# A row-sum kernel on one core: its first 8 MB loaded by two DMAs of 64 partitions instead of one of 128

## The chip, the core and the metric

The kernel runs on one core of a Trainium2 chip. The time is the device time of one execution in microseconds (us), the median of three runs. VectorE is DVE in the profile, ScalarE is ACT, GpSimd is POOL, SyncE is SP, and SyncE's queue of DMA issues is SPq. TensorE is not used.

## What is computed

```
x: [32, 512, 1024] float32
relu_x = np.maximum(x, 0)
return np.sum(relu_x, axis=-1)        # [32, 512] float32
```

That is 16,384 rows of 1,024 numbers, 67.1 MB in, and one number per row out, 65.5 KB.

## The kernel before

The rows are laid on the 128 partitions of the on-chip memory. A partition takes 16 consecutive rows at a time, which is one contiguous stretch of 64 KB in DRAM. Seven loads of 8 MB (128 stretches of 64 KB each, `ROWS = 16`) go in turn into three buffers (`NBUF = 3`, tiles `io0` to `io2`). A last block of 8 MB comes in smaller loads: 8 rows per partition, 4 rows, and then four rows cut into pieces that get smaller towards the end.

All loads are issued by SyncE (helper `load`, line 103), in order, on its one queue. From the fourth on, a load waits until VectorE has finished with the buffer that it overwrites (the tuple in `freed`). Each load has a semaphore of its own, which stands at 16 once its data are there.

The first block is worked on in the simplest way: ScalarE loads its activation table (line 142) and clamps the whole buffer in place (`clamp`, line 144), then VectorE sums all its rows (`total`, line 152). The table load carries ScalarE's wait for the first load. Later blocks are cut in two halves of 8 or 7 rows for these two steps, and from the sixth block on some rows are done in one instruction each, which clamps and sums: on ScalarE (`act_row`, line 159) or on VectorE (`dve_row`, line 167). The last four rows are shared out by columns among ScalarE, VectorE and GpSimd (lines 121, 126, 234, 254).

The sums gather in the tile `res`, one column per row of a partition. Three stores, all on SyncE's queue behind the loads (helper `store`, wait at line 114, issue at line 115), bring them out: the first block's 16 columns, all the others but two, and the last two.

The order of instructions is written out by hand: there is no scheduler. `open_without_barrier` takes the first `EARLY` instructions of SyncE, which are loads, and puts them into the program's opening block, ahead of all else that SyncE does. At the end SyncE clears the semaphores.

The first block has its own views of the arrays, `xf` and `of`; all other blocks use `xv` and `ov`. In both, partition p holds 16 consecutive rows.

Of the kernel before, what the change touches and what calls it, by code (L numbers as in the profile page):

```python
# [5 lines left out]
RELU = mybir.ActivationFunctionType.Relu  # L6
MAX, ADD = mybir.AluOpType.max, mybir.AluOpType.add
P = 128

ROWS = 16  # L10
NBUF = 3
# [13 lines left out]
LAST_DVE, LAST_ACT = 252, 151  # L25
MIDDLE_ACT, END_ACT = 214, 321

EARLY = 1


def kernel(tc: tile.TileContext, x: bass.AP, out: bass.AP):
    nc = tc.nc
    sems = Semaphores(tc)

    tc.close()
    tc.compile()
    nc.cur_bb = nc.bb_map[tc.start_bb_name]
    body = nc.cur_bb.bb.instructions
    ends = list(body)
    body.clear()  # L40
    n_stores = relu_sum(nc, sems, x, out)
    body.extend(ends)


    nc.cur_bb = nc.bb_map[tc.start_bb_name + "_end"]
    nc.cur_bb.bb.instructions.clear()
    nums = sorted(s.num for s in (*sems.loads, sems.act, sems.dve))
    cleared = range(nums[0], nums[-1] + 1)
    assert len(cleared) == len(nums)
    nc.sync.sem_clear(cleared)  # L50
    nc.sync.wait_ge(sems.stored, 16 * n_stores).then_inc(sems.stored, -16 * n_stores)
    open_without_barrier(tc, EARLY)


class Semaphores:
    def __init__(self, tc: tile.TileContext):
        n = len(TWO) + len(TAIL) + 4
        self.loads = [tc.alloc_semaphore(f"load{i}") for i in range(n)]
        self.act = tc.alloc_semaphore("act")
        self.dve = tc.alloc_semaphore("dve")  # L60
        self.end = self.loads[-1]
        self.stored = tc.alloc_semaphore("stored")


def relu_sum(nc, sems: Semaphores, x: bass.AP, out: bass.AP):
    x_flat = x.flatten_outer_dims()
    N, D = x_flat.shape
    NT = N // P
    NB = len(TWO)
    assert N == P * NT == P * ROWS * (NB + 1)  # L70
    assert sum(TAIL) == ROWS - 4
    assert HEAD + MIDDLE + LAST_DVE == D and HEAD == 2 + LAST_DVE

    bufs = [nc.alloc_sbuf_tensor(f"io{i}", [P, ROWS, D], F32) for i in range(NBUF)]
    res = nc.alloc_sbuf_tensor("res", [P, NT], F32)


    n_last = LAST_DVE + LAST_ACT
    last = nc.alloc_sbuf_tensor("last", [P, 2 + n_last + 2], F32)


    N1 = P * ROWS
    xf = x_flat[:N1].rearrange("(p m) d -> p m d", p=P)
    xv = x_flat[N1:].rearrange("(p m) d -> p m d", p=P)
    o_flat = out.rearrange("b s -> (b s)")
    of = o_flat[:N1].rearrange("(p m) -> p m", p=P)
    ov = o_flat[N1:].rearrange("(p m) -> p m", p=P)

    def rows(m, n):
        if m < ROWS:  # L90
            return xf[:, m : m + n, :]
        return xv[:, m - ROWS : m - ROWS + n, :]

    def sums(m, n):
        if m < ROWS:
            return of[:, m : m + n], res[:, m : m + n]
        return ov[:, m - ROWS : m - ROWS + n], res[:, m : m + n]

    n_load = n_act = n_dve = n_store = 0
# [1 line left out]
    def load(dst, src, after=None):  # L101
        nonlocal n_load
        dma = nc.sync.dma_start(out=dst, in_=src)  # L103
        if after:
            dma.wait_op(sems.dve, after[1], "sem-ge")
        dma.then_inc(sems.loads[n_load], 16)
        n_load += 1
        return sems.loads[n_load - 1]

    def store(m, n, act, sem, count):  # L110
        nonlocal n_store
        dst, src = sums(m, n)
        if act:
            nc.sync.wait_ge(sems.act, act)
        nc.sync.dma_start(out=dst, in_=src).wait_op(sem, count, "sem-ge").then_inc(
            sems.stored, 16
        )
        n_store += 1

    def act_part(ap, accum_out, after):  # L120
        nc.scalar.activation(out=ap, in_=ap, func=RELU, accum_out=accum_out).wait_op(  # L121
            *after, "sem-ge"
        ).then_inc(sems.end, 1)
# [15 lines left out]
    def clamp(ap, loaded):  # L139
        nonlocal n_act  # L140
        if n_act == 0:
            nc.scalar.preload_act_table(RELU).wait_op(loaded, 16, "sem-ge")  # L142
            loaded = None
        i = nc.scalar.activation(out=ap, in_=ap, func=RELU)  # L144
        if loaded is not None:
            i.wait_op(loaded, 16, "sem-ge")
        i.then_inc(sems.act, 1)
        n_act += 1

    def total(ap, m, n):  # L150
        nonlocal n_dve
        nc.vector.tensor_reduce(  # L152
            out=res[:, m : m + n], in_=ap, axis=mybir.AxisListType.X, op=ADD
        ).wait_op(sems.act, n_act, "sem-ge").then_inc(sems.dve, 1)
        n_dve += 1

    def act_row(ap, accum_out, loaded):
        nonlocal n_act
        i = nc.scalar.activation(out=ap, in_=ap, func=RELU, accum_out=accum_out)  # L159
        if loaded is not None:  # L160
            i.wait_op(loaded, 16, "sem-ge")
        i.then_inc(sems.act, 1)
        n_act += 1

    def dve_row(ap, accum_out, loaded):
        nonlocal n_dve
        i = nc.vector.tensor_scalar(  # L167
            out=ap,
            in0=ap,
            scalar1=0.0,  # L170
            scalar2=None,
            op0=MAX,
            op1=ADD,
            accum_out=accum_out,
        )
        if loaded is not None:
            i.wait_op(loaded, 16, "sem-ge")
        i.then_inc(sems.dve, 1)
        n_dve += 1

    freed = []
    m = 0
    for j in range(NB):
        buf = bufs[j % NBUF]
        loaded = load(buf[:, :, :], rows(m, ROWS), j >= NBUF and freed[j - NBUF])
        c = 0
        act_waits = dve_waits = loaded
        for n in TWO[j]:
            clamp(buf[:, c : c + n, :], act_waits)
            total(buf[:, c : c + n, :], m + c, n)  # L190
            act_waits = None
            c += n
        for _ in range(ACT[j]):
            act_row(buf[:, c, :], res[:, m + c : m + c + 1], act_waits)
            act_waits = None
            c += 1
        for _ in range(DVE[j]):
            dve_row(buf[:, c, :], res[:, m + c : m + c + 1], dve_waits)
            dve_waits = None
            c += 1  # L200
        assert c == ROWS
        freed.append((n_act, n_dve))
        m += ROWS


    buf = bufs[NB % NBUF]
    c = 0
    for n in TAIL:
        loaded = load(
            buf[:, c : c + n, :], rows(m, n), None if c else freed[NB - NBUF]  # L210
        )
        for i in range(n):
            if i % 2 == 0 or (n == 8 and i == 7):
                act_row(buf[:, c, :], res[:, m : m + 1], loaded if i == 0 else None)
            else:
                dve_row(buf[:, c, :], res[:, m : m + 1], loaded if i == 1 else None)
            c += 1
            m += 1

    flat = buf[:, :, :].rearrange("p c d -> p (c d)")  # L220
    src = rows(m, 4).rearrange("p c d -> p (c d)")
    at = c * D
    head = 2 * D + HEAD
# [4 lines left out]
    loaded = load(flat[:, at : at + head], src[:, :head])  # L228
    act_row(buf[:, c, :], res[:, m : m + 1], loaded)
    sums_act = n_act  # L230
    dve_row(buf[:, c + 1, :], res[:, m + 1 : m + 2], loaded)
    sums_dve = n_dve
    clamped = flat[:, at + 2 * D : at + head]
    nc.gpsimd.tensor_scalar(  # L234
        out=clamped, in0=clamped, scalar1=0.0, scalar2=None, op0=MAX
    ).wait_op(loaded, 16, "sem-ge").then_inc(sems.end, 1)
    for lo, hi, n, first, second in (
# [3 lines left out]
        loaded = load(flat[:, at + lo : at + hi], src[:, lo:hi])  # L241
        act_part(flat[:, at + lo : at + lo + n], last[:, first : first + 1], (loaded, 16))
        dve_part(flat[:, at + lo + n : at + hi], last[:, second : second + 1], (loaded, 16))
    loaded = load(last[:, 2 : 2 + n_last], src[:, middle:end])
    assert loaded is sems.end

    store(0, ROWS, freed[0][0], sems.dve, freed[0][1])
    store(ROWS, NT - ROWS - 2, sums_act, sems.dve, sums_dve)  # L250


    all_there = (sems.end, 16 + 5)
    nc.vector.scalar_tensor_tensor(  # L254
        out=clamped,
# [5 lines left out]
        accum_out=res[:, NT - 2 : NT - 1],  # L261
    ).wait_op(*all_there, "sem-ge").then_inc(sems.end, 1)
    act_part(last[:, 2 + LAST_DVE :], res[:, NT - 1 : NT], all_there)
    store(NT - 2, 2, 0, sems.end, 16 + 5 + 2)
    return n_store


def open_without_barrier(tc: tile.TileContext, n_loads: int):

    SP = mybir.EngineType.SP
    blocks = tc.nc.main_func.blocks
    opening = blocks[0].instructions
    body = next(b for b in blocks if b.name == tc.start_bb_name).instructions
    for i in list(opening):
        if isinstance(i, (mybir.InstDrain, mybir.InstEventSemaphore)):
            opening.remove(i)
    loads = [i for i in body if i.engine == SP][:n_loads]
    for i in loads:  # L280
        assert isinstance(i, mybir.InstDMACopy)
        body.remove(i)
    at = next(n for n, i in enumerate(opening) if i.engine == SP)
    opening[at:at] = loads
# [30 lines left out]
```

## Time and profile before

| | |
|---|---|
| time, median of 3 runs (lowest to highest) | 160.98 us (160.91 to 160.99) |
| profiled execution, first to last instruction (span) | 159.7 us |
| VectorE busy | 118.8 us (74%) |
| ScalarE busy | 103.6 us (65%) |
| GpSimd busy | 1.0 us (1%) |
| the 16 DMA engines busy, mean | 98.0% |
| moved | 67.18 MB, 421 GB/s over the span |

The span is the time that the profile gives for its own execution, and no timed run belongs to it; the runs' median lies 1.28 us above it, which is what lies around the first and the last instruction. In the lines of the profile, a group names its line in the kernel, the engine, the operation and the tiles (`out<-in`). The timeline gives start and duration in us, and in brackets the idle time before an instruction and what ended it. The waits give, for each pair, the total, the number and the longest. The chain of waits is followed back from the last instruction to whatever released each step. The DMA part gives the size of an issue and the time from its issue to its landing. Beside these views the trace has a record of every DMA packet: when it started, how long it took and how many bytes it had.

### The profile page before, as it was taken

The numbers are of one execution on the slowest core, as the hardware profiler recorded it, in microseconds if no ns is written. First come the engines' busy times: TensorE is split into PE (matmuls) and PEld (weight loads), VectorE is DVE, ScalarE is ACT, GpSimd is POOL, SyncE is SP. The second block draws the span as 40 slices with busy tenths as digits, with TensorE's granted clock in tenths as the row PEclk, the third lists the DMA queues.
The fourth block names the chain that finished last, engine by engine and source line by source line (L and its number), as shares of the span: only waits on it lengthen the run. The fifth ranks groups of instructions, "written<-read, shape, count | busy, mean of one in ns | idle before, by whom it ended". The sixth has DMA issues, their size and how long they took to land.

```text
span 159.7 us, 125 instructions
## 1 busy us (share of the span) xinstructions
DVE 118.8 (74%) x44; ACT 103.6 (65%) x53; POOL 1.0 (1%) x5
## 2 busy tenths in 40 slices
DVE  0000000006999799999999999999999799999986
ACT  0000049993699808996099951999329993496995
POOL 0000000000000000000000000000000000000001
DMA  7996996996997997979969969969969969898993
GB/s 263 525 525 263 525 509 279 525 509 279 525 476 312 525 443 345 525 328 460 525 279 509 525 263 525 525 263 525 509 279 525 492 295 525 353 435 386 407 409 128
DMA packets 2304, 67.18 MB, mean 421 GB/s; under 512 B 640, under 2 KB 768, under 8 KB 1024
## 3 DMA queue, kind: packets, MB, share of 16 engines
q1 hardware_dynamic: 2304, 67.18, 98.0%
HBM read 67.11 MB, written 0.07 MB: 421 GB/s over the span
## 4 chain that ended last, share of the span: by engine, by line
DVE 45%; DMA 45%; ACT 9%; SPq 1%; issue 0%
DMA io<-in_x_dram 45%; DVE res L152 43%; ACT io L144 9%; DVE io L167 1%; SPq L103 1%; DVE io L126 1%; DVE io L254 0%
## 5 line engine op out<-in xcount | busy, mean ns | idle before, releaser
L152 DVE TENSOR_REDUCE res<-io 128x8 f32<-128x8192 f32 (+2 forms) x10 | 101.1, 10175 | 38.9 <-ACT io L144 38.9
L144 ACT ACTIVATE io<-io 128x8192 f32<-128x8192 f32 (+2 forms) x10 | 81.8, 8218 | 25.9 <-DMA io<-in_x_dram 25.9
L159 ACT ACTIVATE io<-io 128x1024 f32<-128x1024 f32 x18 | 18.8, 1043 | 6.6 <-DMA io<-in_x_dram 6.6
L167 DVE TENSOR_SCALAR_CACHE_REDUCE io<-io 128x1024 f32<-128x1024 f32 x14 | 16.2, 1214 | 0.5 <-DMA io<-in_x_dram 0.4
L142 ACT ACT_TABLE_LOAD x1 | 1.3, 1283 | 22.0 <-DMA io<-in_x_dram 22.0
L159 ACT ACTIVATION_READ_ACCUMULATOR io<-io 128x1 f32 x18 | 3.4, 187 | 0.0
L234 POOL TENSOR_SCALAR io<-io 128x254 f32<-128x254 f32 x1 | 0.8, 840 | 155.1 <-DMA io<-in_x_dram 155.1
L167 DVE DVE_READ_ACCUMULATOR io<-io 128x1 f32 x14 | 1.1, 82 | 0.0
L126 DVE TENSOR_SCALAR_CACHE_REDUCE io<-io 128x552 f32<-128x552 f32 (+1 forms) x2 | 1.1, 596 | 0.0
L121 ACT ACTIVATE io<-io 128x321 f32<-128x321 f32 (+1 forms) x2 | 0.9, 426 | 0.1
L254 DVE SCALAR_TENSOR_TENSOR io<-last,io 128x254 f32<-128x254 f32 x1 | 0.4, 425 | 0.0
L121 ACT ACTIVATION_READ_ACCUMULATOR io<-io 128x1 f32 x2 | 0.4, 187 | 0.0
L121 ACT ACTIVATE last<-last 128x153 f32<-128x153 f32 x1 | 0.3, 332 | 0.0
L121 ACT ACTIVATION_READ_ACCUMULATOR last<-last 128x1 f32 x1 | 0.2, 187 | 0.0
L126 DVE DVE_READ_ACCUMULATOR io<-io 128x1 f32 x2 | 0.2, 84 | 0.0
L299 POOL MEMSET const-bfloat16-1.0<- 128x1 bf16 x1 | 0.1, 101 | 0.0
L299 POOL MEMSET const-uint8-127<- 128x1 uint8 x1 | 0.1, 101 | 0.0
L299 POOL MEMSET const-float32-0.0<- 128x1 f32 x1 | 0.1, 99 | 0.2 <-issue 0.2
L299 POOL MEMSET const-float32-1.0<- 128x1 f32 x1 | 0.1, 98 | 0.0
L254 DVE DVE_READ_ACCUMULATOR io<-last,io 128x1 f32 x1 | 0.1, 83 | 0.0
## 6 DMA issues: line engine op xcount, KB each, us to landing
io<-in_x_dram SPq DMA_DIRECT2D x1, 4096.0 KB, 23.8
io<-in_x_dram SPq DMA_DIRECT2D x1, 2048.0 KB, 28.3
io<-in_x_dram SPq DMA_DIRECT2D x1, 1151.0 KB, 30.6
io<-in_x_dram SPq DMA_DIRECT2D x1, 436.5 KB, 31.2
io<-in_x_dram SPq DMA_DIRECT2D x1, 259.0 KB, 31.4
last<-in_x_dram SPq DMA_DIRECT2D x1, 201.5 KB, 31.4
io<-in_x_dram SPq DMA_DIRECT2D x7, 29.1
out_dram<-res SPq DMA_DIRECT2D x1, 55.0 KB, 1.6
```

What stands on the lines that cost most here:

```text
L103: dma = nc.sync.dma_start(out=dst, in_=src)
L121: nc.scalar.activation(out=ap, in_=ap, func=RELU, accum_out=accum_out).wait_op(*after, "sem-ge").then_inc(sems.end, 1)
L126: i = nc.vector.tensor_scalar(out=ap, in0=ap, scalar1=0.0, scalar2=None, op0=MAX, op1=ADD, accum_out=accum_out,)
L142: nc.scalar.preload_act_table(RELU).wait_op(loaded, 16, "sem-ge")
L144: i = nc.scalar.activation(out=ap, in_=ap, func=RELU)
L152: nc.vector.tensor_reduce(out=res[:, m : m + n], in_=ap, axis=mybir.AxisListType.X, op=ADD).wait_op(sems.act, n_act, "sem-ge").then_inc(se ...
L159: i = nc.scalar.activation(out=ap, in_=ap, func=RELU, accum_out=accum_out)
L167: i = nc.vector.tensor_scalar(out=ap, in0=ap, scalar1=0.0, scalar2=None, op0=MAX, op1=ADD, accum_out=accum_out,)
L234: nc.gpsimd.tensor_scalar(out=clamped, in0=clamped, scalar1=0.0, scalar2=None, op0=MAX).wait_op(loaded, 16, "sem-ge").then_inc(sems.end, 1)
L254: nc.vector.scalar_tensor_tensor(out=clamped, in0=last[:, : 2 + LAST_DVE], scalar=0.0, in1=clamped, op0=MAX, op1=ADD, accum_out=res[:, NT ...
L299: nc = _bacc.Bacc("TRN2", target_bir_lowering=False, num_devices=1)
```

## The change

The first 8 MB come in two loads on SyncE's queue instead of one. The 128 stretches of 64 KB are counted off as 16 groups of 8. The first load takes the first four stretches of each group and puts them on partitions 0 to 63; the second takes the other four and puts them on partitions 64 to 127. The view `xf` is laid out for that: 16 groups `e`, two halves `h`, four stretches `i`. Both loads stand in the opening block (`EARLY = 2`). The second one has a new semaphore, `half`, for which ScalarE waits before it goes on to its wait for the first. ScalarE's clamp and VectorE's sum of the block are as they were, over all 128 partitions.

Since the rows of the first block now lie on other partitions, its sums go out by two stores of 64 partitions each, through a view `of` of the same layout. All else stays.

```diff
+H = P // 2
...
-EARLY = 1
+EARLY = 2
...
-    xf = x_flat[:N1].rearrange("(p m) d -> p m d", p=P)
+    xf = x_flat[:N1].rearrange("(e h i m) d -> h e i (m d)", h=2, e=16, m=ROWS)
...
-    of = o_flat[:N1].rearrange("(p m) -> p m", p=P)
+    of = o_flat[:N1].rearrange("(e h i m) -> h e i m", h=2, e=16, m=ROWS)
...
-    def store(m, n, act, sem, count):
+    def store(dst, src, act, sem, count):
         nonlocal n_store
-        dst, src = sums(m, n)
         if act:
             nc.sync.wait_ge(sems.act, act)
...
-        loaded = load(buf[:, :, :], rows(m, ROWS), j >= NBUF and freed[j - NBUF])
+        if j == 0:
+            loaded = load(buf[:H, :, :], xf[0])
+            nc.sync.dma_start(out=buf[H:, :, :], in_=xf[1]).then_inc(sems.half, 16)
+            nc.scalar.wait_ge(sems.half, 16)
+        else:
+            loaded = load(buf[:, :, :], rows(m, ROWS), j >= NBUF and freed[j - NBUF])
...
-    store(0, ROWS, freed[0][0], sems.dve, freed[0][1])
-    store(ROWS, NT - ROWS - 2, sums_act, sems.dve, sums_dve)
+    store(of[0], res[:H, :ROWS], freed[0][0], sems.dve, freed[0][1])
+    store(of[1], res[H:, :ROWS], 0, sems.dve, freed[0][1])
+    store(*sums(ROWS, NT - ROWS - 2), sums_act, sems.dve, sums_dve)
...
-    store(NT - 2, 2, 0, sems.end, 16 + 5 + 2)
+    store(*sums(NT - 2, 2), 0, sems.end, 16 + 5 + 2)
```

## The prediction, made before the change was run

> **What bounds the kernel now.** I read the page first: the span, the busy shares and the DMA part.
>
> ```profile
> span 159.7 us, 125 instructions
> DVE 118.8 (74%) x44; ACT 103.6 (65%) x53; POOL 1.0 (1%) x5
> ...
> DMA packets 2304, 67.18 MB, mean 421 GB/s; under 512 B 640, under 2 KB 768, under 8 KB 1024
> ## 3 DMA queue, kind: packets, MB, share of 16 engines
> q1 hardware_dynamic: 2304, 67.18, 98.0%
> ```
>
> Neither compute engine is full; the sixteen DMA engines are, at 98.0% of their time. The missing 2% is 3.2 us: the start and the end. The chain of waits, in order of time, looks different at first sight:
>
> ```profile
> 0.43 40.86 DMA io<-in_x_dram
> 41.30 0.02 issue
> 41.32 13.87 ACT io L144
> 55.19 0.02 issue
> 55.21 68.79 DVE res L152 x7
> ...
> 124.87 30.59 DMA io<-in_x_dram
> 155.46 0.02 issue
> 155.48 1.23 DVE io L167 x2
> ```
>
> It runs over VectorE for 69 us because a load from the fourth on is issued when VectorE has freed a buffer. But these loads are issued early: the waits of SyncE's queue and the DMA part say by how much.
>
> ```profile
> SPq L103 <- DVE res L152: 121.3, 5, 53.1
> ...
> io<-in_x_dram SPq DMA_DIRECT2D x7, 29.1
> ```
>
> A load lands a median 29.1 us after its issue, and moving its 8 MB takes less, as the timeline shows:
>
> ```profile
> 21.99 1.28 ACT L142 ACT_TABLE_LOAD   x1 [21.99 <-DMA io<-in_x_dram]
> 23.29 13.86 ACT L144 ACTIVATE io<-io 128x16384 f32<-128x16384 f32 x1
> 37.17 17.22 DVE L152 TENSOR_REDUCE res<-io 128x16 f32<-128x16384 f32 x1 [37.17 <-ACT io L144]
> 41.32 13.86 ACT L144 ACTIVATE io<-io 128x16384 f32<-128x16384 f32 x1 [4.18 <-DMA io<-in_x_dram]
> ```
>
> Load 0 is there at 21.99 and load 1 at 41.32: 19.33 us for 8.39 MB. So a load queues about 10 us behind others. The one refill that matters for the start is load 3: VectorE ends its first reduction at 37.17 + 17.22 = 54.39, and the three loads issued at the start last until 21.99 + 2 x 19.33 = 60.65, 6.3 us later. From the start of an issue to the first packet it takes 1.0 us (packet records of load 0), so some 5 us of cover are left. Hence every us by which the first 8 MB land later or sooner moves every later landing, the last one at 155.46, and the end.
>
> The packet records give the rate of one engine. Of 896 packets of 64 KB, 742 took 2.415 to 2.421 us. Smaller ones took 1.213 (32 KB), 0.347 (9,208 B) and 0.068 us (1,612 B): 8.8 ns plus 27.21 bytes per ns. Sixteen engines at 27.21 make 435 GB/s, and 8 packets of 2.418 make the 19.34 us of a load.
>
> **The change part by part.**
>
> *The first load becomes two on 64 partitions each.* Bytes and size of stretches stay; every engine has four 64 KB packets for partitions 0 to 63, then four for 64 to 127. SyncE's queue is served in order, so all sixteen engines write into the lower half of the partitions together, then all into the upper half. No instruction of the trace loads onto fewer than 128 partitions, so I bound the price from both sides. Lower bound: the 27.21 bytes per ns belong to the engine. Then a half takes what the nearest equal-sized load takes, the 4 MB one of the tail: it landed at 147.79 and the load before it at 138.08, 9.71 us, and both halves take 19.4, as now. Upper bound: the limit belongs to the way into the partitions, 435 GB/s over 128 of them. Then 64 partitions take in 217.7 GB/s, an engine's packet lasts 2 x 2.418 = 4.84 us, a half 4 x 4.84 = 19.34 and the two 38.7: 19.34 us more. The stores obey the same line (440 B: 25 ns; 8.8 + 440/27.21 = 25.0), so the limit lies in something that both directions use, which the memory that is read from HBM need not be: the engine or the partitions' side. In rows, that is nearly an even choice. What tips it is the start: fifteen engines begin their first packet between 1.02 and 1.46 us and take 2.80 to 3.30 us for it; the sixteenth begins at 2.04, alone, and takes 2.415. So engines that do the same thing together do hinder each other somewhere; their ways aren't all their own. I take the upper bound, and keep both for the range.
>
> [...] No run so far shows a load on 64 partitions.
>
> *SyncE's issues.* One more load at the start; issues follow each other there by 0.43 to 0.47 us (0.383 us for the first, 0.43 for the next two). The second half is issued at about 0.43, some 9 us before an engine has done its first four packets. Loads 1 and 2 are issued 0.45 us later behind 19 us or more of queued data: nothing. With that cover gone it would be 0.45 us.
>
> *One more completion per engine*: one packet of 4 bytes, 9 ns on each engine: 0.01 us.
>
> *ScalarE waits for the second half's semaphore before the table load.* Behind it stand its table load and all of its clamps, and VectorE behind them. ScalarE is idle up to 21.99 anyway and needs both halves; the added wait costs 0.02 us (the "issue" steps of the chain), covered by the 4.18 us in which ScalarE waits for load 1. With 64-partition loads at half rate this wait ends 19.3 us later; the clamp of load 1 still waits for its data, and load 3 still has its 5 us, because all of these shift together.
>
> *The first store becomes two*, 4 KB each, the same 128 packets of 64 B at 11 ns. The first is issued at 126.91 (0.40 us), the second right behind it; then SyncE waits 29.3 us for ScalarE's last sums (line 114). That hides the 0.40, and it would cost it in full without that gap. The packets themselves follow the last load's on each engine, as now.
>
> *Fewer packets in the first hand-out.* If the stretched first packets come from handing out 8 stretches to every engine, 4 would start faster. The engine that lies last ended its first packet at 4.71, the others at 4.10 to 4.46. Bounds: nothing, or at most what all engines would gain by starting at 1.46 and taking 2.42: 4.71 - 3.88 = 0.83 us. The nearest row for the hand-out speaks for little: in the last store, 128 packets and 16 completions on idle engines are over in 0.2 us (159.09 to 159.28). In the forecast this gain, if any, lies beneath the doubled first packets, so I put it at 0.
>
> Sum, against the profiled execution: span 159.7 + 19.34 - 0 + 0.01 = 179.05 us. The runs' median, 160.98, lies 1.28 above that span; the same 1.28 on top gives **180.3 us**.
>
> **The rivals.**
>
> *No effect.* The rate is the engine's; halves take 9.7 us each, the rest is hidden. For it: one rate for all engines and packet sizes. Against it: the stretched first packets. 161.0 us.
>
> *Faster: the start.* Same premise, and the shorter hand-out lets the slowest engine start earlier. Because that engine sets each landing by about 0.25 us to the end (completions of load 1: fifteen from 40.32 to 40.69, the last at 40.94), its gain is the kernel's. Half of the bound, 0.42 us: 160.6. It decides if halves run at the full rate and that engine's first packet ends by 4.39, that is 0.32 sooner. For it: start and end are all of the 2% that the DMA engines do not work. Against it: the store's 0.2 us for as many packets.
>
> *A little slower.* Full rate, but the second hand-out falls upon running packets. Some of the trace's 64 KB packets take up to 2.485 instead of 2.418; eight of these are 0.54 us: 161.5.
>
> *Half rate, shared unevenly.* If one engine of a pair goes first, it moves on to the upper half while the other writes the lower: three turns of 9.67 instead of four, +9.7 us: 170.6. That is within the forecast's case.
>
> That the change does not do what it says would need the halves on other partitions or out of order; the diff's slices `buf[:H]` and `buf[H:]` on one queue leave no room for it.
>
> **How the numbers follow.** About 0.2% (0.32 us) can be told from no change. Half rate 0.58 (mostly even sharing); no effect 0.14; a little slower 0.12; faster by the start 0.16. Faster 0.16, same 0.14, slower 0.58 + 0.12 = 0.70. The likeliest case's own range is 170.6 to 181.0. The range must also hold no effect and a little slower (0.84 in all), so it begins at 160.98 - 0.32, rounded to 160.6, and ends at 181.0: the sum plus 0.7 us for a first packet as stretched as now.
>
> **What would show it.** Right: ScalarE's table load starts at about 41.3 instead of 21.99; the page's GB/s stands near 218 for the first 39 us; 64 KB packets of load 0 take about 4.84 us and of load 1 again 2.42; loads 0 and 1 still land some 19.3 us apart; the last data arrive at about 174.8, and DMA's mean falls to about 375 GB/s. Wrong: a table load at 21.5 to 22.5 us, with packets of 2.42 us from the first halves on: then the rate is the engine's, and only the time of the first landing against 21.99 is left to decide the sign. A first landing at 31 to 32 us would mean uneven sharing. A gap in the DMA part ahead of load 3 would mean that the 5 us of cover did not hold.

## The result, and the profile after

The changed kernel takes 182.13 us (182.11 to 182.42), the one before 160.99 beside it: 1.1319 times as long, 95% interval 1.1303 to 1.1335. The predicted 180.3 has the direction and the half rate of the first 8 MB; the range ended at 181.0, 1.1 us too low.

The page of the changed kernel begins:

```profile
span 180.6 us, 128 instructions
...
DMA  9999994999978999999799999978999999799895
GB/s 232 232 232 232 232 232 87 189 189 465 465 334 363 465 465 465 465 465 436 319 407 465 465 465 465 465 319 377 465 465 465 465 465 407 319 436 465 370 404 169
DMA packets 2336, 67.18 MB, mean 372 GB/s; under 512 B 672, under 2 KB 800, under 8 KB 1056
## 3 DMA queue, kind: packets, MB, share of 16 engines
q1 hardware_dynamic: 2336, 67.18, 98.1%
```

The engines count as busy for 98.1% of their time, as before (98.0%), yet in the first nine slices (40.6 us) they move half of what they move later. So a busy engine is not an engine at its rate: a packet of 64 KB that takes 5.07 us instead of 2.42 (packet records, below) counts as busy all the while. The sums by stretch of time, the last two columns being the DMA engines' busy share and GB/s, say the same without the slices. Before, from 6 to 11 us:

```profile
core 0: us, DVE busy (x) ACT busy (x) POOL busy (x), PEclk, DMA share, GB/s
6.00:11.00 5.00, 0.00 (x0) 0.00 (x0) 0.00 (x0) 1.00 0.97 419
```

and after, in the same stretch, during load 1 and later on:

```profile
6.00:11.00 5.00, 0.00 (x0) 0.00 (x0) 0.00 (x0) 1.00 1.01 210
...
44.00:60.00 16.00, 1.92 (x1) 14.04 (x2) 0.00 (x0) 1.00 1.06 459
64.00:140.00 76.00, 75.24 (x8) 54.30 (x8) 0.00 (x0) 1.00 0.99 429
```

From 44 us on the rate is back (packets are counted where they start, so that a short stretch can stand a little high). The timeline of the changed kernel has the two early issues and what waits for their data:

```profile
0.00 0.68 SPq L101 DMA_DIRECT2D io<-in_x_dram  x1
...
0.73 0.58 SPq L184 DMA_DIRECT2D io<-in_x_dram  x1
...
42.90 1.28 ACT L139 ACT_TABLE_LOAD   x1 [42.90 <-DMA io<-in_x_dram]
44.19 13.86 ACT L141 ACTIVATE io<-io 128x16384 f32<-128x16384 f32 x1
58.08 17.22 DVE L149 TENSOR_REDUCE res<-io 128x16 f32<-128x16384 f32 x1 [58.08 <-ACT io L141]
62.17 13.86 ACT L141 ACTIVATE io<-io 128x16384 f32<-128x16384 f32 x1 [4.12 <-DMA io<-in_x_dram]
...
81.52 13.95 ACT L141 ACTIVATE io<-io 128x8192 f32<-128x8192 f32 x2 [5.50 <-DMA io<-in_x_dram]
100.87 13.95 ACT L141 ACTIVATE io<-io 128x8192 f32<-128x8192 f32 x2 [5.40 <-DMA io<-in_x_dram]
```

The table load starts at 42.90 instead of 21.99. Load 1 is there 19.27 us later, as before (19.33), and loads 2 and 3 follow at 81.52 and 100.87. (The second block, too, is clamped and summed whole; it is from the third on that blocks are cut in halves.) The chain of waits, from there on, is the one of before with every step moved:

```profile
76.06 68.79 DVE res L149 x7
...
145.71 30.60 DMA io<-in_x_dram
176.31 0.02 issue
176.34 1.23 DVE io L164 x2
```

The reductions take the same 68.79 us, and the last load's data come at 176.31 instead of 155.46, 20.85 later. Nothing was lost and nothing won back after the first 8 MB.

The packet records, sorted by which packet followed which, give the price (means over the sixteen engines, us):

| an engine's packet of 64 KB | before | after |
|---|---|---|
| start of the first | 1.25 | 1.57 |
| 1st | 3.05 | 4.84 |
| 2nd to 4th, 6th to 8th, each | 2.42 | 5.07 |
| 5th (the first for partitions 64 to 127) | 2.42 | 4.88 |
| 9th (the first of load 1) | 2.42 | 2.78 |
| from the 10th on | 2.42 | 2.42 |

The differences add up to 0.32 + 1.79 + 6 x 2.65 + 2.46 + 0.36 = 20.8, and the records' own mean end of load 1 moved from 40.53 to 61.40: 20.87. The span grew by 20.9.

### The profile page after: what moved, and what is told of

It reads as the page before. It is cut to its first block, busy times and chain, and to the rows that moved or that the text cites. A ratio compares the mean times of both kernels' runs of the same rounds, so it can differ in the third digit from the quotient of the medians.

```text
span 180.6 us, 128 instructions
## 1 busy us (share of the span) xinstructions
DVE 118.8 (66%) x44; ACT 103.5 (57%) x53; POOL 1.0 (1%) x5
## 3 DMA queue, kind: packets, MB, share of 16 engines
q1 hardware_dynamic: 2336, 67.18, 98.1%
## 4 chain that ended last, share of the span: by engine, by line
DMA 40%; DVE 40%; ACT 16%; another core or an unknown queue 2%; SPq 1%; issue 0%; ACTq 0%
DMA io<-in_x_dram 40%; DVE res L149 38%; ACT io L141 15%; SPq L101 1%; ACT L139 1%; DVE io L164 1%; DVE io L123 1%; DVE io L257 0%; ACTq L185 0%
```

## Is it the partitions? Experiments 1, 2, 3 and 11

All experiments change only how the first 8 MB are loaded (and, where rows change places, how their sums are stored). Except in experiment 5, load 1 queues right behind. ScalarE waits for every load that is added. In the pieces of code below, a minus line is one of the changed kernel (in experiment 11, of experiment 2), and lines that only follow from the ones shown are left out.

**Theory W**: which partitions a load has decides its rate, because on some sets of partitions the engines meet two by two and take turns (the prediction's 2 x 2.418 us, measured as 5.07), and on others they do not. Where the expectations speak of a way, they mean the place where engines would meet. That there are such places, and which partitions would belong to one, is not shown; the runs show times alone. Rivals: the order in DRAM; an even share for each single partition, which is how the prediction's upper bound reckoned; or the mere second load.

*Experiment 1* reads each half from one contiguous 4 MB (`xf` as before the change) and has one store. By W, packets take 5.07 us again, and the time is 181.7 to 182.2 us:

```diff
-            loaded = load(buf[:H, :, :], xf[0])
-            nc.sync.dma_start(out=buf[H:, :, :], in_=xf[1]).then_inc(sems.half, 16)
+            loaded = load(buf[:64, :, :], xf[:64])
+            nc.sync.dma_start(out=buf[64:, :, :], in_=xf[64:]).then_inc(sems.part[0], 16)
```

> The two loads of 64 partitions stay, but each reads one contiguous 4 MB of DRAM and the store stays whole. [...] Rival R (the changed order of the reads from DRAM halves the rate): packets of 2.42, first landing about 22, time 161.0. If the longer first issue (0.68 us instead of 0.38) comes from the three-step view of DRAM, it is 0.38 here and all lies 0.3 us earlier than in the changed kernel.

182.45 us (1.1332 times before, 1.1317 to 1.1348). Packets from the second on took 5.12 us, but for the fifth with 4.95. The order of the reads is not the cause; if anything it made 5.07 out of 5.12. The first issue took 0.55 us (0.68 in the changed kernel, 0.38 before), so that a little of the longer issue came from the three-step view of DRAM, and most of it came with the load on 64 partitions.

*Experiment 2* takes 64 other partitions first. That engines do not meet on these was the author's estimate. W then gives the first load four packets of 2.42 us on each engine and the two loads of 32 partitions two of 5.07 each, 9.7 + 2 x 10.1 instead of 19.3 us, so +10.6 us and a time of about 171.6:

```diff
+            loaded = load(buf[32:96, :, :], xf[32:96])
+            nc.sync.dma_start(out=buf[:32, :, :], in_=xf[:32]).then_inc(sems.part[0], 16)
+            nc.sync.dma_start(out=buf[96:, :, :], in_=xf[96:]).then_inc(sems.part[1], 16)
```

> The first block in three loads: partitions 32 to 95, then 0 to 31, then 96 to 127. [...] Rival P (each partition takes in 3.4 GB/s, whichever it is): first load 4.84 us per packet, the loads of 32 partitions 9.7 us per packet: 58 us instead of 19.3, time about 199.7. Rival R (order in DRAM): about 161.

172.03 us (1.0689 times, 1.0674 to 1.0704), against 171.6 forecast by W. The sums by stretch of time, in the first load and in the second:

```profile
6.00:11.00 5.00, 0.00 (x0) 0.00 (x0) 0.00 (x0) 1.00 0.97 419
...
13.00:18.00 5.00, 0.00 (x0) 0.00 (x0) 0.00 (x0) 1.00 1.02 210
```

64 partitions at the full 419 GB/s: it is not their number. Its packets after the first took 2.42 us, those for 0 to 31 and for 96 to 127 5.12 (but 4.30 to 4.70 for the first one for 0 to 31, and 4.91 for the first one for 96 to 127). Rival P, the even share, falls.

In experiments 1 and 2 the number of a stretch in DRAM is the number of its partition. *Experiment 11* parts them:

```diff
-            loaded = load(buf[32:96, :, :], xf[32:96])
-            nc.sync.dma_start(out=buf[:32, :, :], in_=xf[:32]).then_inc(sems.part[0], 16)
+            loaded = load(buf[32:96, :, :], xf[:64])
+            nc.sync.dma_start(out=buf[:32, :, :], in_=xf[64:96]).then_inc(sems.part[0], 16)
```

> The three loads of the run with partitions 32 to 95 first, but these 64 partitions now get the first 4 MB of DRAM (which came at half rate when they went to partitions 0 to 63); 0 to 31 get the next 2 MB. Theory W (the partitions decide): first load 2.42 us per packet, time 171.9 as in that run. Rival R2 (the place in DRAM decides; in the runs so far with three loads the number of the stretch and of the partition were the same): the first load at 5.1, time about 182 or more.

172.39 us (timed once), and from 6 to 11 us:

```profile
6.00:11.00 5.00, 0.00 (x0) 0.00 (x0) 0.00 (x0) 1.00 0.97 419
```

The same 4 MB of DRAM that came at half rate in experiment 1 come at full rate. The partitions decide.

*Experiment 3* has two loads, but on all 128 partitions:

```diff
+            loaded = load(buf[:, :8, :], xf[:, :8, :])
+            nc.sync.dma_start(out=buf[:, 8:, :], in_=xf[:, 8:, :]).then_inc(sems.part[0], 16)
```

> The first block in two loads of 8 rows each on all 128 partitions, 32 KB packets. Theories W, P and R: full rate, packets of 1.213 us, time 161.0 within 0.3 (one more completion per engine, 16 packets of 1.213 instead of 8 of 2.418: +0.07 us per engine; the first packets may end sooner by up to 0.8). Rival N (any second load in the first block costs the 20 us, by its hand-out or its wait): 182.

160.95 against 160.96 us (1.0004 times, 0.9995 to 1.0013). A second load, its semaphore, and ScalarE's second wait cost nothing that can be measured in the whole time. Its span is a little shorter (159.4 to 159.9, against 159.5 to 160.0), and the time around the span some 1.47 us instead of 1.33.

*Experiment 8* is experiment 3 with `EARLY = 1`, to see whether the second early load makes those 0.15 us or so:

> The two loads of 8 rows on all partitions, with only the first in the opening block. In the run with both in it the span was some 0.1 us shorter than before but the time around the span 0.15 us longer (1.45 instead of 1.30). Theory: the second early load costs what lies outside the span: 160.8. Rival: the extra time outside comes from the added load and semaphore themselves: 160.95 again.

161.05 against 161.01 us (1.0011 times, 1.0002 to 1.0020), with 1.45 to 1.60 around the span. So the theory falls: the 0.15 us come with the added load and its semaphore, wherever the load stands. Where they lie within the time around the span, the profile does not show. No version beat the kernel before.

## What sharing costs: experiments 5, 10, 7 and 4

If two engines take turns, two packets one after the other make 4.84 us, but a packet took 5.07. Are these 5% a slower way or the sharing?

*Experiment 5* lets only eight engines work: four loads of 32 partitions whose DRAM view has 8 groups outermost (`xq[0]` to `xq[3]`), and load 1 issued when all have landed.

```diff
+    xq = x_flat[:N1].rearrange("(e q i m) d -> q e i (m d)", q=4, e=8, m=ROWS)
...
+            loaded = load(buf[0:32, :, :], xq[0])
...
+            if j == 1:
+                for sem in (sems.loads[0], *sems.part):
+                    nc.sync.wait_ge(sem, 16)
```

> The first block in four loads of 32 partitions, each on 8 engines (DRAM view with 8 groups outermost), and load 1 is issued only when all four have landed, so that these 8 engines have the chip to themselves for the first block. Theory W, sharing costs extra: with one engine per way all 64 KB packets take 2.42 us in all four loads, 9.7 us a load, 38.7 in all; the 5.07 to 5.13 of two engines on one way is then 4.8 to 6% more than twice the undisturbed packet, and this extra belongs to the sharing. Time about 182 (38.7 instead of 19.3, and some 1.5 us in which load 1 starts from an empty queue). Rival F (a way itself passes only 25.6 bytes per ns for some partitions): packets of 2.56. Rival E (the 8 engines reach some partitions badly, which is what made both groups take 5.12 in the run with eight engines): 5.1 in the loads for 0 to 31 or 96 to 127, and a time of 192 or more.

183.68 us (timed once). The sums by stretch of time:

```profile
6.00:11.00 5.00, 0.00 (x0) 0.00 (x0) 0.00 (x0) 1.00 0.48 210
```

Half of the engines are idle (0.48), and 210 GB/s flow, as much as in the changed kernel with all sixteen busy (1.01). After each engine's first one (3.0 to 3.6 us), the packets took 2.42 us in all four loads, but for a single one of 2.68. In the changed kernel the second eight engines add nothing, and the 8 MB even take a little longer than here (the table load starts at 41.87 here, at 42.90 there). So the 5% is a price of sharing. W stands so far; rival F (a slower way) and rival E (partitions that these engines reach badly) fall.

*Experiment 10* has eight loads of 16 partitions, one behind the other, with one stretch for each engine. On the 32 partitions of experiment 2 a packet took 5.12 us, 2.12 times one alone; that four engines meet on 16 is the author's estimate, by twice the crowding:

```diff
+            loaded = load(buf[0:16, :, :], xf[0:16])
...
```

> [...] Theory W with a loss that grows with the number that meets (2: 5.07 to 5.13 us, that is 1.05 times two packets; 3: 8.36 in the load of partitions 80 to 127, 1.15 times three packets): 4 x 2.42 = 9.7 us at least and up to some 12 us with the loss, 78 to 96 us for the block, time 220 to 238. Rival: the loss is a fixed 4 to 6% of a shared way: 10.1 to 10.3 us, time 223 to 225. Rival P (each partition its own 3.4 GB/s): 16 partitions take in 54 GB/s, 19.3 us per packet, time about 295.

215.81 us (timed once), below all that was expected: the packets from the second on took 9.30 us, 3.85 times 2.418. Sixteen engines moved 16 x 65,536 B in 9.30 us, 112.7 GB/s onto 16 partitions. That four engines meet there, or three on the 48 partitions of experiment 6's last load with 8.36 us, no run shows; if four do, four packets in turn would make 9.67 us, and 9.30 is less. So the loss does not grow with the crowding. Nor is it that 32 partitions take in no more: eight engines brought 8 x 65,536 B onto them in 2.42 us, 216.6 GB/s (experiment 5), sixteen at 5.12 only 204.8 (experiment 2). Why sharing loses 5% stays open.

*Experiment 7* is the changed kernel with the second half issued from ScalarE's queue (and `EARLY = 1`):

```diff
-            nc.sync.dma_start(out=buf[H:, :, :], in_=xf[1]).then_inc(sems.half, 16)
+            nc.scalar.dma_start(out=buf[H:, :, :], in_=xf[1]).then_inc(sems.half, 16)
```

> The changed kernel with the second half issued by ScalarE on its own queue, right at its start, and only the first load in the opening block. Theory W with order: SyncE's one queue makes all engines write to the same half at a time; with two queues an engine has packets for both halves waiting, so the halves are mixed and the first landing comes sooner: between 22 and 42.9 us, time between 161.5 and 182. If engines take the two queues in turn and in step, nothing is gained: 182. Rival (two loads of 64 partitions cost what they cost, whatever their order): 182.

181.18 us (1.1244 times, 1.1228 to 1.1259). The DMA part shows both queues at work:

```profile
q1 hardware_dynamic: 2256, 62.98, 87.1%
q10 hardware_dynamic: 80, 4.19, 10.9%
```

The packet records show why that gains so little: all sixteen engines take one packet from the one queue and one from the other, in step (starts at 6.05 to 7.11 us on q10, 10.93 to 11.99 on q1, 15.81 to 16.86 on q10). So at any time they are still in the same half. But each packet after an engine's first, now always the first after a change of half, took 4.87 to 4.92 us, as the changed kernel's fifth did: little more than 4.84. So the 5% is seen only on packets that follow one into the same half.

*Experiment 4* is like experiment 5, but load 1 is not held back, and only the lower half is cut so: it comes in two loads of 32 partitions on eight engines, the upper half in one load on sixteen. The 181 us take it that the eight engines keep to 2.42 us a packet on the lower half and that all sixteen take 5.07 once they are on the upper half together.

```diff
+            loaded = load(buf[:32, :, :], xq[0])
+            nc.sync.dma_start(out=buf[32:64, :, :], in_=xq[1]).then_inc(sems.part[0], 16)
+            nc.sync.dma_start(out=buf[64:, :, :], in_=xf).then_inc(sems.part[1], 16)
```

> The lower 64 partitions come in two loads of 32 whose DRAM view has 8 groups outermost, so that 8 engines carry them with 8 stretches each; the upper 64 in one load on 16 engines. Theory W, with one engine per way: packets of the 8 engines take 2.42 us though these are 64 partitions, so the 4 MB take 19.4 us on half of the engines, as long as on all of them in the changed kernel (20.3); the other 8 engines go on meanwhile at 2.42. [...] Time about 181. Rival P: with eight engines 64 or 32 partitions still take in only 3.4 GB/s each: two loads of 2.1 MB at 109 GB/s, packets of 4.84. If the extra 4.8% (5.07 against 2 x 2.418) comes from two engines sharing, there is none of it in the first 20 us here.

203.82 us (timed once). The eight engines had packets of 5.12 us for partitions 0 to 31 once the other eight had begun on the upper half, that is on other partitions; 2.42 while those were in the first packets of load 1; and 6.1 to 8.4 when the eight themselves went on to the upper half. Neither these packets nor the 22.8 us over the expected 181 follow from W alone, so that the next question is what engines do to others.

## Do engines that meet hold up others? Experiments 6, 9, 12, 13 and 14

These five differ in one number, the first partition `a` of the first load of 64; the other two loads take the rest.

```diff
+            loaded = load(buf[a : a + 64, :, :], xf[a : a + 64])
+            nc.sync.dma_start(out=buf[:a, :, :], in_=xf[:a]).then_inc(sems.part[0], 16)
+            nc.sync.dma_start(out=buf[a + 64 :, :, :], in_=xf[a + 64 :]).then_inc(sems.part[1], 16)
```

An engine has four of the 64 stretches. With `a = 32` all sixteen took 2.42 us for each from the second on (experiment 2). Experiment 6 has `a = 16`. That eight engines meet there, at 5.1 us, and eight do not, at 2.42, was the author's estimate for W:

> The first block in three loads: partitions 16 to 79, then 0 to 15, then 80 to 127. [...] Rival P (each partition has its own share of the rate) or any limit on the whole load: all sixteen alike, 4.8 to 5.1. Time some 11 to 20 us over before.

All sixteen took 5.10 to 5.13. Experiment 9 has `a = 28`, where the author's estimate was one pair of engines that meets. Theory C: such a pair sets the pace of all sixteen, at about 5.1 us; theory U: no engine holds up another, fourteen go at 2.42 and two at 5.1.

> The first block in three loads: partitions 28 to 91, then 0 to 27, then 92 to 127. [...] Time 20 to 35 us over before either way, since the two smaller loads run on fewer engines and ways.

Fourteen took 2.42 us, two 5.05 to 5.13, and the time was 32.9 us over before. (On how many engines the smaller loads ran no run shows.) Experiments 12, 13 and 14 have `a = 24`, `a = 20`, and, on the other side, `a = 36`. Counted on from no slow engine at 32 and two at 28, each step of 4 would add two slow engines, a pair that meets: two pairs at 24, three at 20, four at 16, and one at 36. The expectations count so:

> [...] With one pair (28 to 91) the other fourteen ran at 2.42; with four pairs (16 to 79) all sixteen took 5.1. Theory G (engines that meet block others once enough of them do): either 12 engines at 2.42 and 4 at 5.1, or all at 5.1, with the turn between two and four pairs. [...]

> [...] Theory G: 10 engines at 2.42 and 6 at 5.1, or all at 5.1 if three pairs are enough to block the others. Together with the runs for one, two and four pairs this says where the turn is.

> [...] If one pair leaves the others alone wherever it lies: 14 engines at 2.42, two at 5.1. Rival: the run from 28 to 91 was special to its pair or its engines, and all sixteen take 5.1 to 5.2 here, as with two, three and four pairs.

Each was timed once. The 64 KB packets of the first load, from the second on:

| first load | steps of 4 from 32 | engines at 2.42 us | engines at about 5 | time, us |
|---|---|---|---|---|
| 32 to 95 (exp. 2) | 0 | 16 | 0 | 172.03 |
| 28 to 91 | 1 | 14 | 2 (5.05 to 5.13) | 193.84 |
| 36 to 99 | 1 | 14 | 2 (4.92 to 5.23) | 190.02 |
| 24 to 87 | 2 | 0 | 16 (5.07 to 5.23) | 201.62 |
| 20 to 83 | 3 | 0 | 16 (5.06 to 5.12) | 201.68 |
| 16 to 79 | 4 | 0 | 16 (5.10 to 5.13) | 195.90 |

(The whole times also hold the two smaller loads, which are cut differently each time, and do not compare with one another.) The sums by stretch of time for 28 to 91:

```profile
6.00:11.00 5.00, 0.00 (x0) 0.00 (x0) 0.00 (x0) 1.00 0.97 393
```

and for 16 to 79:

```profile
6.00:11.00 5.00, 0.00 (x0) 0.00 (x0) 0.00 (x0) 1.00 1.02 210
```

393 GB/s one step from 32, 210 four steps from it. One step away exactly two engines are slow, on either side of 32. But experiment 6, of which eight engines at 2.42 were expected, has none, and from two steps on all sixteen engines take 5.06 to 5.23 us, also those that, counted on from the first step, would meet no other (twelve with two steps). So neither theory of experiment 9 holds, that one pair sets the pace of all (C) or that no engine holds up another (U); of G, the others are blocked once enough engines meet, and the turn lies between one and two steps. What in the chip holds the others up, or whether all sixteen meet there, isn't shown by these runs. In the changed kernel it decides nothing, because all sixteen engines take 5.07 us there anyway. It would explain experiment 4 if the second eight engines met among themselves on the upper half. The records name neither an engine nor its partitions, so this is argued only, and that something else acts in experiment 4 is not excluded.

## The prediction, point by point

**What bounds the kernel.** Right: each us by which the first 8 MB came later moved the end by one (20.91 us at the table load, 20.85 at the last data). The 5 us of cover for load 3 held: load 3 was issued after VectorE's first reduction (58.08 + 17.22 = 75.30), 6.2 us before load 2 was there, and loads 2 and 3 still landed 19.35 us apart (81.52 and 100.87).

**The upper bound for the halves.** Right that the limit lies on the partitions' side (experiments 2 and 11), but not in how it shares: the working spread 435 GB/s evenly over 128 partitions, and 32 to 95, as many as 0 to 63, took in the full 419. The halves of this change came at half rate (210 of 419 GB/s), and so the fraction came out right; why these partitions do and 32 to 95 do not is not shown. The signs that were named for it came: the table load at 42.90 us (41.3 named), 210 GB/s (218), packets of 5.07 us (4.84) and of 2.42 again in load 1, the last data at 176.31 (174.8). The hint that tipped the choice, the stretched first packets at the start, was no evidence: in experiment 2 the first packets of a load without sharing were just as stretched (2.44 to 3.26 us), and so were those of the eight engines of experiment 5. Nor did the sixteenth engine run alone in its 2.415 us (2.04 to 4.46): the others were in theirs until 4.10 at least. From the rows, then, the choice of the upper bound was luck.

**The term that was mis-sized** is "an engine's packet lasts 2 x 2.418 = 4.84 us". Sharing is not free: six of eight packets took 5.07, 6 x 0.237 = 1.42 us more, and why sharing loses these 5% stays open. The other terms of 20.87 - 19.34 = 1.53 nearly cancel: the first packets' old stretch went under in the longer ones (1.79 more instead of 2.42, -0.62), the fifth packet took 0.05 more, the first packet of load 1 still met others (+0.36), and the first packet began 0.32 later.

**SyncE's issues**, put at nothing: the second one is hidden as said, but the first one itself took 0.68 instead of 0.383 us, as a first load on 64 partitions took longer to issue in all runs (0.55 to 0.61 us with a plain view in experiments 1, 2 and 6, against 0.38 in experiment 3 on 128). Why isn't shown; the number of partitions alone is not it, for the one on 16 in experiment 10 took 0.39. Nothing covers the first issue.

**The 1.28 us around the span**, carried over unchanged, became 1.52: 0.24 us, of which experiments 3 and 8 show some 0.15 with any added load. With the 1.53 this makes the 1.8 us between 180.3 and 182.13.

**Faster by the start**: wrong on its own ground too. Experiment 2's first load hands out 64 stretches at full rate, and its first packets ended at 4.38 to 4.73 us, against 4.10 to 4.71 before; they began 0.33 us later, behind a longer issue, and took as long (3.01 us on average, against 3.05). **Uneven sharing** did not happen: the second to fourth packets of all engines took 5.05 to 5.09 us. ScalarE's wait, the 4-byte packets and the second store cost the end nothing that the trace shows, as expected. (One count was off: 747, not 742, of the 896 packets lie between 2.415 and 2.421 us; nothing hangs on it.)

## What to carry to other kernels

Cut a load by rows and keep all 128 partitions (experiment 3: 160.95 against 160.96 us); if it must be cut by partitions, time the very piece: which partitions it has counted here, not how many (0 to 63 came at 210 GB/s, 32 to 95 at 419). The busy share of the DMA engines did not show their rate (1.01 at 210 GB/s, 0.97 at 419): compare the GB/s of the stretch, or one packet's time, with those of an undisturbed stretch. When a resource is shared, the plain fraction is an estimate, and the range must hold more on both sides: sixteen engines on partitions 0 to 63 took 2.10 times as long for a packet here, on 16 partitions 3.85 times.

## What was not expected of the hardware

- On partitions 24 to 87 all sixteen engines take 5.07 to 5.23 us a packet; on 28 to 91 and on 36 to 99 two are slow (4.92 to 5.23) and fourteen stay at 2.42.
- Sixteen engines on 16 partitions take 9.30 us a packet, 3.85 times the 2.42 of an engine undisturbed; on 0 to 63, or on 32 partitions, 5.07 to 5.12, 2.10 to 2.12 times.
- Eight engines, on 32 partitions at a time, bring as many GB/s as sixteen do on 64 (210), in packets of 2.42 instead of 5.07 us.
- A first load on 64 partitions took SyncE 0.55 to 0.68 us to issue, one on 128 took 0.38, one on 16 took 0.39.
